# Inverting the delta rule's triangles in four row units, and merging their blocks in four queue steps

## The chip, the cores and the metric

One core of a Trainium2 chip runs the whole network once. The metric is the time of one execution on the device, in microseconds (us), as the median of several runs.

## What is computed

The network has two decoder layers on 256 tokens of width 2048. The first layer is a gated DeltaNet layer with 16 heads, the second attends differentially with a shared K/V; each ends with an MLP. The change lies in the DeltaNet layer, whose core the reference writes as

```python
lower = jnp.where(strict, jnp.einsum('bhnid,bhnjd->bhnij', k_beta, k) * decay, 0.0)
tri = lower + jnp.eye(CHUNK, dtype=lower.dtype)
sol = lax.linalg.triangular_solve(tri, rhs, left_side=True, lower=True, unit_diagonal=True)
```

The kernel does it with blocks of 128 tokens instead of 64: for each of 16 heads and 2 blocks there is one unit triangular matrix of 128x128 that has to be inverted and applied.

## The kernel before

Most of the program is weight products. A call of `gemm` multiplies the 256 tokens by 1024 columns of a weight matrix. The fp32 weights arrive in tiles of 128x1024 (`wr`), ScalarE rounds each to a high part `wh` (line 78), VectorE takes the remainder `wl` (line 79), and TensorE adds three products per tile, token block and half of the columns (lines 191 to 193, 128x512 each). One call has 16 weight tiles, 2 token blocks and 2 column halves, so 16 x 2 x 2 x 3 = 192 of these **weight matmuls**. Weight tiles are loaded four at a time; there are six buffers each for `wh` and `wl`.

The DeltaNet layer takes its heads in two halves of eight (`half(0)`, `half(1)`), and each half calls `gemm` for its k, q and v. All that is not a weight product is side work, and two queues hold it. `self.units` holds convolutions, scores and the like; `self.chain` holds steps that depend on each other: the inverse and the solve. `pump`, called after each token block of each four weight tiles, so once per 24 weight matmuls, takes one step of the chain and then `rate` units. The side work of a half therefore runs beside the weight products of its own v and of the next calls.

The inverse of a half, lines 571 to 644, is this chain: `inv_gather` copies the 32x32 diagonal blocks of 16 triangles (8 heads, 2 token blocks) through DRAM to 64 partitions; three empty steps; `inv_rows` inverts them there by forward substitution, two VectorE instructions per row (lines 593 and 600), 31 rows, in six units of up to six rows; `inv_scatter` writes the results back through DRAM into the diagonal of `Z` (lines 608 and 611, GpSimd's DMA queue); two empty steps; `inv_flip` transposes `Z` to `Y` (line 614); one empty step; and `inv_merge` puts pairs of blocks together, 32 to 64 and 64 to 128, in one step. For each pair it multiplies by `U` (line 630), copies the product from PSUM with ScalarE (line 631), multiplies again (line 634), and negates into `Y` with VectorE (line 635); for the first pairs a third product goes to `Z` (lines 641, 642). The products touch 32 or 64 rows and columns of the 128x128 array: a quarter or a smaller block of it, given by where the operands lie.

After the merge come two `solve` steps of four heads each: a product with `Y` (line 655), a ScalarE copy (656), a product (660), a VectorE subtraction (661), a product (664), a copy (665), and then the output products (670, 672), of which ScalarE sums the squares (677).

A scheduler of the framework turns this into one fixed order of instructions per engine when the program is built: it follows the order of the code, and by its own estimate of times it lets instructions that it thinks ready go ahead. The hardware runs each engine's instructions in that order, and an instruction that has to wait holds up all behind it on its engine.

Of the kernel before, what the change touches and what calls it, by code (L numbers as in the profile page):

```python
# [14 lines left out]
ALU = mybir.AluOpType  # L15
# [3 lines left out]
P = 128  # L19
# [3 lines left out]
KD = D // P  # L23
DFF = 8192
C = 1024
G = 512
# [9 lines left out]
class Trunk:  # L36
# [292 lines left out]
    @staticmethod  # L329
    def ends(n):  # L330

        return [5, 5, 6] if n == D // C - 1 else None
# [45 lines left out]
    def gated_deltanet(self, x, w_in, conv_w, a_log, dt_bias, norm_w, w_out, g, b, out=None):  # L378
# [6 lines left out]
        nc = self.nc  # L385
        v_ = nc.vector
        NH, DK, HH = 16, 128, 8
# [198 lines left out]
        def inv_rows(hf, j0, j1):  # L586
            Gp = hf["inv"][:64, :C].rearrange("p (j i) -> p j i", j=32)
            X = hf["inv"][:64, C:].rearrange("p (i c) -> p i c", i=32)
            for j in range(j0, j1):
                n = 31 - j  # L590
                t0 = j % 2 * 256
                t = hf["t"][:64, t0 : t0 + n * (j + 1)].rearrange("p (i c) -> p i c", i=n)
                v_.tensor_tensor(
                    t,
                    Gp[:, j, j + 1 :].unsqueeze(2).broadcast_to([64, n, j + 1]),
                    X[:, j : j + 1, : j + 1].broadcast_to([64, n, j + 1]),
                    op=ALU.mult,
                )
                xs = X[:, j + 1 :, : j + 1]
                v_.tensor_tensor(xs, xs, t, op=ALU.subtract)  # L600

        def inv_scatter(hf):
            X = hf["inv"][:64, C:].rearrange("p (i c) -> p i c", i=32)
            hf["Z"] = self.blk()
            nc.gpsimd.memset(hf["Z"], 0.0)
            Zv = hf["Z"].rearrange("p (n c) -> p n c", c=P)
            buf = self.dram.tile([4, 2 * HH, 32, 32], F32, name="g_inverses")
# [4 lines left out]
        def inv_flip(hf):  # L612
            hf["Y"] = self.blk()
            v_.transpose(hf["Y"], hf["Z"])

        def inv_merge(hf):

            Z = hf["Z"].rearrange("p (n c) -> p n c", c=P)
            Y = hf["Y"].rearrange("p (n c) -> p n c", c=P)
            U = lambda n: hf["U1"][:, n] if n < HH else hf["UA2"][:, 0, n - HH]  # L620
            mm = nc.tensor.matmul
            for w, r0 in ((32, 0), (32, 64), (64, 0)):
                a, b_ = slice(r0, r0 + w), slice(r0 + w, r0 + 2 * w)
                per = G // w
                for n0 in range(0, 2 * HH, per):
                    N = range(n0, n0 + per)
                    cs = lambda n: slice((n - n0) * w, (n - n0 + 1) * w)
                    tp, ts = self.ps(), self.sm()
                    for n in N:
                        mm(tp[b_, cs(n)], U(n)[a, b_], Z[a, n, a], start=True, stop=True)  # L630
                    nc.scalar.copy(ts[b_], tp[b_])
                    yp = self.ps()
                    for n in N:
                        mm(yp[a, cs(n)], ts[b_, cs(n)], Y[b_, n, b_], start=True, stop=True)
                    v_.tensor_scalar(
                        Y[a, n0 : n0 + per, b_], yp[a].rearrange("p (n c) -> p n c", c=w), -1.0, None, op0=ALU.mult
                    )
                    if w == 32 and r0 == 0:
                        zp = self.ps()
                        for n in N:  # L640
                            mm(zp[b_, cs(n)], Y[b_, n, b_], ts[b_, cs(n)], start=True, stop=True)
                        v_.tensor_scalar(
                            Z[b_, n0 : n0 + per, a], zp[b_].rearrange("p (n c) -> p n c", c=w), -1.0, None, op0=ALU.mult
                        )

        def solve(hf, gi, H):

            Y = hf["Y"].rearrange("p (n c) -> p n c", c=P)
            rv = hf["r"]
# [38 lines left out]

        def start_inverse(hf):
            rest = [(lambda *a: None, (hf,))]  # L690
            rows = [(lambda hf, j=j: inv_rows(hf, j, min(j + 6, 31)), (hf,)) for j in range(0, 31, 6)]
            self.chain.extend([(inv_gather, (hf,))] + rest * 3 + rows)
            self.chain.extend([(inv_scatter, (hf,))] + rest * 2 + [(inv_flip, (hf,))] + rest + [(inv_merge, (hf,))])

        def start_solve(hf, H):
            self.chain.extend((solve, (hf, g_, H)) for g_ in range(NG))
# [1 line left out]
        def half(hh):  # L698
            hf, H = {}, hh * HH
# [38 lines left out]
            for name, c0, ct in (("k", D, 16), ("q", 0, 0), ("v", 2 * D, 32)):  # L738
                pre = None
                if hh == 0 and name == "k":  # L740
                    pre = constants
                if hh == 0 and name == "q":
                    pre = gates
                self.gemm(KD, self.cols(w_in, c0 + H * DK), self.x_stat, ev_for(name, ct + H), pre=pre, rate=2)

        def gate(n):
            def ev(gi, t, ps):
# [9 lines left out]
            return ev  # L757

        half(0)
        half(1)  # L760
        for n in range(2):
            self.gemm(
# [204 lines left out]
```

## Time and profile before

| what | value |
|---|---|
| median of 3 runs | 2448.11 us (2443.59 to 2451.93) |
| the profiled execution's own time | 2446.75 us |
| its span in the profile | 2445.0 us |
| TensorE busy | 2406.5 us, 98% |
| VectorE busy | 1494.4 us, 61% |
| ScalarE busy | 1080.3 us, 44% |
| GpSimd busy | 48.3 us, 2% |
| mean granted clock of TensorE | 0.995 |

In the views, PE is TensorE's matmuls, PEld its weight loads, DVE VectorE, ACT ScalarE, POOL GpSimd, SP SyncE. The DeltaNet layer's six calls for k, q, v of both halves lie between about 11 and 301 us (half 0 and k, q of half 1) and up to 365 us (v of half 1); z follows up to 484 us. The merge and solves of half 0 stand from 262.8 to 293 us, those of half 1 from 440.8 to 478 us. A small fp32 product shows as two records.

### The profile page before, as it was taken

The page shows a single profiled execution, that of the slowest core. Times are in us where ns is not written, and L with a number is a line of the kernel's source. Part 1 is how long each engine was busy: PE and PEld are TensorE (multiplying, and loading weights), DVE is VectorE, ACT ScalarE, POOL GpSimd, SP SyncE. Part 2 cuts the span into 40 slices and gives each one's busy share as a digit, 9 for nine tenths or more (in the row PEclk, how much of TensorE's full clock was granted, in tenths as well). Part 3 has the DMA queues.
Part 4 walks back from the last instruction along what each step waited for, and adds up shares of the span by engine and source line. Part 5 has one row for each costly group of instructions (what it writes and reads, how often), then busy time and mean ns, then how long its engine had stood idle before and what let it go on. Part 6 is the DMA issues. An engine that isn't in the chain of part 4 may idle for free.

```text
span 2445.0 us, 30450 instructions
## 1 busy us (share of the span) xinstructions
PE 2406.5 (98%) x11492; PEld 1976.3 (81%) x11492; DVE 1494.4 (61%) x2348; ACT 1080.3 (44%) x1474; POOL 48.3 (2%) x79
## 2 busy tenths in 40 slices
PE   8999999999999999999999999999999999999997
PEld 6888888787888888888887877777888888888886
DVE  4789789557545554545557565766754545554556
ACT  4545445434433443534443454544343443443442
POOL 0010020000000000000000000000000000000001
PEclk9999999999999999999999999999999999999999
DMA  6545445464565556565554545555455555656553
GB/s 231 156 134 174 123 132 178 155 236 159 182 203 190 181 191 212 180 216 178 201 193 145 191 144 167 161 173 198 143 186 196 186 193 177 219 182 214 184 195 121
DMA packets 120212, 438.85 MB, mean 179 GB/s; under 512 B 13760, under 2 KB 13792, under 8 KB 119040
## 3 DMA queue, kind: packets, MB, share of 16 engines
q1 hardware_dynamic: 115920, 420.79, 52.1%
q0 software_dynamic: 2560, 11.13, 1.5%
q10 hardware_dynamic: 1584, 4.98, 0.5%
q8 instruction: 90, 1.47, 0.2%
q14 instruction: 58, 0.48, 0.1%
HBM read 433.70 MB, written 3.15 MB: 179 GB/s over the span
## 4 chain that ended last, share of the span: by engine, by line
PE 90%; DVE 5%; DMA 2%; issue 1%; ACT 1%; SPq 0%; ACTq 0%; DVEq 0%; POOLq 0%
PE acc L191 27%; PE acc L192 27%; PE acc L193 27%; PE ps L221 3%; DVE wl L79 1%; PE ps L832 1%; DMA wr<-in_gdn_w_in_dram 1%; PE ps L563 1%; ACT wh L78 1%; DMA wr<-in_shared_w_kv_dram 1%; PE ps L498 1%; PE ps L860 0%; PE ps L871 0%; DVE blk L282 0%; DVE blk L600 0%
## 5 line engine op out<-in xcount | busy, mean ns | idle before, releaser
L79 DVE TENSOR_TENSOR wl<-wr,wh 128x1024 fp32r<-128x1024 f32 x785 | 951.2, 1222 | 670.1 <-ACT wh L78 627.6
L78 ACT CAST wh<-wr 128x1024 fp32r<-128x1024 f32 x785 | 817.1, 1053 | 914.6 <-PE acc L193 748.3
L191 PE MATMUL acc<-wh,xhl 128*128 128x512 f32 x1860 | 737.0, 396 | 0.0
L192 PE MATMUL acc<-wl,xhl 128*128 128x512 f32 x1860 | 731.0, 393 | 0.1
L193 PE MATMUL acc<-wh,xhl 128*128 128x512 f32 x1860 | 729.0, 392 | 0.0
L191 PE MATMUL acc<-wh,blk 128*128 128x512 f32 x1280 | 499.3, 390 | 0.0
L193 PE MATMUL acc<-wh,blk 128*128 128x512 f32 x1280 | 498.6, 390 | 0.0
L192 PE MATMUL acc<-wl,blk 128*128 128x512 f32 x1280 | 498.5, 389 | 0.0
L191 PEld LDWEIGHTS acc<-wh,xhl 128*128 128x128 f32 x1860 | 351.0, 189 | 70.9 <-issue 1.7
L193 PEld LDWEIGHTS acc<-wh,xhl 128*128 128x128 f32 x1860 | 350.1, 188 | 71.7
L192 PEld LDWEIGHTS acc<-wl,xhl 128*128 128x128 f32 x1860 | 350.9, 189 | 69.4 <-issue 1.0
L193 PEld LDWEIGHTS acc<-wh,blk 128*128 128x128 f32 x1280 | 240.3, 188 | 50.2
L191 PEld LDWEIGHTS acc<-wh,blk 128*128 128x128 f32 x1280 | 240.3, 188 | 49.6
L192 PEld LDWEIGHTS acc<-wl,blk 128*128 128x128 f32 x1280 | 240.4, 188 | 49.3
L310 DVE SCALAR_TENSOR_TENSOR blk<-blk,acc 128x512 f32<-128x512 f32 x80 | 54.6, 684 | 71.3 <-PE acc L193 71.3
L221 PE MATMUL ps<-ident,sm 128*128 128x128 f32 x512 | 81.3, 275 | 2.1 <-DVE sm L882 1.7
L221 PEld LDWEIGHTS ps<-ident,sm 128*128 128x128 f32 x512 | 61.3, 140 | 26.8 <-PE acc L193 7.5
L78 ACT CAST blk<-ps 128x512 fp32r<-128x512 f32 x80 | 46.8, 585 | 70.2 <-PE ps L221 70.2
L362 DVE TENSOR_TENSOR sm<-sm 128x512 f32<-128x512 f32 x64 | 44.1, 691 | 50.5 <-ACT sm L361 50.1
L79 DVE TENSOR_TENSOR blk<-ps,blk 128x512 fp32r<-128x512 f32 x80 | 54.9, 686 | 30.1 <-ACT blk L78 30.1
L361 ACT ACTIVATE sm<-acc 128x512 f32<-128x512 f32 x64 | 38.3, 599 | 63.3 <-PE acc L193 60.4
L484 DVE SCALAR_TENSOR_TENSOR sm<-blk,g_cw,sm 128x255 f32<-128x255 f32 (+2 forms) x144 | 60.9, 475 | 0.0
(209 smaller groups left out, 1123.5 us busy)
## 6 DMA issues: line engine op xcount, KB each, us to landing
wr<-in_mlp_w_up_dram SPq DMA_DIRECT2D x256, 512.0 KB, 4.7
wr<-in_mlp_w_down_dram SPq DMA_DIRECT2D x256, 512.0 KB, 5.1
wr<-in_gdn_w_in_dram SPq DMA_DIRECT2D x128, 512.0 KB, 4.3
wr<-in_shared_w_kv_dram SPq DMA_DIRECT2D x64, 512.0 KB, 5.2
wr<-in_gdn_w_out_dram SPq DMA_DIRECT2D x32, 512.0 KB, 5.5
wr<-in_diff_w_q_dram SPq DMA_DIRECT2D x32, 512.0 KB, 4.6
wr<-in_diff_w_o_dram SPq DMA_DIRECT2D x32, 512.0 KB, 4.6
blk<-in_ln_g_dram POOLq DMA_DIRECT2D x4, 1024.0 KB, 7.3
```

The source lines that it names most:

```text
L78: self.nc.scalar.copy(hi, src)
L79: (engine or self.nc.vector).tensor_tensor(lo, src, hi.bitcast(F32), op=ALU.subtract)
L191: mm(ps, xh, wh[:, c], start=(k == 0), stop=False)
L192: mm(ps, xh, wl[:, c], start=False, stop=False)
L193: self.last = mm(ps, xl, wh[:, c], start=False, stop=(k == nk - 1))
L221: self.nc.tensor.transpose(pt[:, i], src[:, i * P : (i + 1) * P], self.ident)
L310: self.nc.vector.scalar_tensor_tensor(rc, rc, alpha, ps, op0=ALU.mult, op1=ALU.add)
L361: self.nc.scalar.activation(a, ps, AF.Relu)
L362: self.nc.vector.tensor_tensor(a, a, a, op=ALU.mult)
L484: v_.scalar_tensor_tensor(y[:, i, d:], u[:, : T - d], w(j), y[:, i, d:], op0=ALU.mult, op1=ALU.add)
L498: nc.tensor.matmul(pn[:, c : c + 1], sq[:, o : o + P], col1, start=True, stop=True)
L563: mm(p1[:, j], kT[:, n, :P], m[:, n], start=True, stop=True)
```

## The change

It does four things. The rows are inverted in four units of up to eight rows instead of six of up to six. The merge is four steps of the chain instead of one: step 0 multiplies by `U` for both pairs of 32 and copies, step 1 does the second products and the negations, steps 2 and 3 do the same for 64. Within a step two sets of products, with a PSUM tile each, are written in turn: for 32 the two sets lie in different quarters of the array, for 64 they are the two token blocks, in one quarter. The empty step ahead of the merge goes. And during the calls for v, `pump` takes three units instead of two.

```diff
--- before.py
+++ after.py
@@ -613,35 +613,51 @@
             hf["Y"] = self.blk()
             v_.transpose(hf["Y"], hf["Z"])
-        def inv_merge(hf):
-            Z = hf["Z"].rearrange("p (n c) -> p n c", c=P)
-            Y = hf["Y"].rearrange("p (n c) -> p n c", c=P)
+        def inv_merge(hf, step):
+            mm = nc.tensor.matmul
+            Z = lambda n: hf["Z"][:, n * P : (n + 1) * P]
+            Y = lambda n: hf["Y"][:, n * P : (n + 1) * P]
             U = lambda n: hf["U1"][:, n] if n < HH else hf["UA2"][:, 0, n - HH]
-            mm = nc.tensor.matmul
-            for w, r0 in ((32, 0), (32, 64), (64, 0)):
-                a, b_ = slice(r0, r0 + w), slice(r0 + w, r0 + 2 * w)
-                per = G // w
-                for n0 in range(0, 2 * HH, per):
-                    N = range(n0, n0 + per)
-                    cs = lambda n: slice((n - n0) * w, (n - n0 + 1) * w)
-                    tp, ts = self.ps(), self.sm()
-                    for n in N:
-                        mm(tp[b_, cs(n)], U(n)[a, b_], Z[a, n, a], start=True, stop=True)
-                    nc.scalar.copy(ts[b_], tp[b_])
-                    yp = self.ps()
-                    for n in N:
-                        mm(yp[a, cs(n)], ts[b_, cs(n)], Y[b_, n, b_], start=True, stop=True)
-                    v_.tensor_scalar(
-                        Y[a, n0 : n0 + per, b_], yp[a].rearrange("p (n c) -> p n c", c=w), -1.0, None, op0=ALU.mult
-                    )
-                    if w == 32 and r0 == 0:
-                        zp = self.ps()
-                        for n in N:
-                            mm(zp[b_, cs(n)], Y[b_, n, b_], ts[b_, cs(n)], start=True, stop=True)
-                        v_.tensor_scalar(
-                            Z[b_, n0 : n0 + per, a], zp[b_].rearrange("p (n c) -> p n c", c=w), -1.0, None, op0=ALU.mult
-                        )
+            w = 32 if step < 2 else 64
+            per = G // w
+            parts = [(0, 0), (64, 0)] if w == 32 else [(0, 0), (0, HH)]
+            ends = lambda r0: (slice(r0, r0 + w), slice(r0 + w, r0 + 2 * w))
+            cs = lambda m: slice(m * w, (m + 1) * w)
+            blocks = lambda p: p.rearrange("p (n c) -> p n c", c=w)
+            def negated(dst, rows, n0, cols, src):
+                d = dst.rearrange("p (n c) -> p n c", c=P)[rows, n0 : n0 + per, cols]
+                v_.tensor_scalar(d, blocks(src[rows]), -1.0, None, op0=ALU.mult)
+            ps = [self.ps() for _ in parts]
+            if step % 2 == 0:
+                hf["ts"] = [self.sm() for _ in parts]
+                for m in range(per):
+                    for (r0, n0), p in zip(parts, ps):
+                        a, b_ = ends(r0)
+                        mm(p[b_, cs(m)], U(n0 + m)[a, b_], Z(n0 + m)[a, a], start=True, stop=True)
+                for (r0, _), p, ts in zip(parts, ps, hf["ts"]):
+                    b_ = ends(r0)[1]
+                    nc.scalar.copy(ts[b_], p[b_])
+                return
+            for m in range(per):
+                for (r0, n0), p, ts in zip(parts, ps, hf["ts"]):
+                    a, b_ = ends(r0)
+                    mm(p[a, cs(m)], ts[b_, cs(m)], Y(n0 + m)[b_, b_], start=True, stop=True)
+            for (r0, n0), p in zip(parts, ps):
+                a, b_ = ends(r0)
+                negated(hf["Y"], a, n0, b_, p)
+            if w == 32:
+                a, b_ = ends(0)
+                zp, ts = self.ps(), hf["ts"][0]
+                for m in range(per):
+                    mm(zp[b_, cs(m)], Y(m)[b_, b_], ts[b_, cs(m)], start=True, stop=True)
+                negated(hf["Z"], b_, 0, a, zp)
         def solve(hf, gi, H):
@@ -688,9 +704,9 @@
         def start_inverse(hf):
             rest = [(lambda *a: None, (hf,))]
-            rows = [(lambda hf, j=j: inv_rows(hf, j, min(j + 6, 31)), (hf,)) for j in range(0, 31, 6)]
+            rows = [(lambda hf, j=j: inv_rows(hf, j, min(j + 8, 31)), (hf,)) for j in range(0, 31, 8)]
             self.chain.extend([(inv_gather, (hf,))] + rest * 3 + rows)
-            self.chain.extend([(inv_scatter, (hf,))] + rest * 2 + [(inv_flip, (hf,))] + rest + [(inv_merge, (hf,))])
+            self.chain.extend([(inv_scatter, (hf,))] + rest * 2 + [(inv_flip, (hf,))] + [(inv_merge, (hf, i)) for i in range(4)])
         def start_solve(hf, H):
             self.chain.extend((solve, (hf, g_, H)) for g_ in range(NG))
@@ -741,7 +757,7 @@
                     pre = constants
                 if hh == 0 and name == "q":
                     pre = gates
-                self.gemm(KD, self.cols(w_in, c0 + H * DK), self.x_stat, ev_for(name, ct + H), pre=pre, rate=2)
+                self.gemm(KD, self.cols(w_in, c0 + H * DK), self.x_stat, ev_for(name, ct + H), pre=pre, rate=3 if name == "v" else 2)
         def gate(n):
             def ev(gi, t, ps):
```

The chain of a half is 16 steps long before and after: two row units and an empty step go, three merge steps come.

What this does to the order shows at three places. The first is **TensorE, the end of half 0's merge and its first solve**. `acc` is the PSUM tile of the weight matmuls, `wh`, `wl` and `xhl` their operands, `ps` the PSUM tile of a side product. Before:

```order
L630 MATMUL ps<-blk 64x64 x8
L193 MATMUL acc<-wh,xhl 128x512
L191 MATMUL acc<-wh,xhl 128x512
L192 MATMUL acc<-wl,xhl 128x512
L193 MATMUL acc<-wh,xhl 128x512
L634 MATMUL ps<-blk,sm 64x64 x8
L655 MATMUL ps<-blk 128x128 x4
L191 MATMUL acc<-wh,xhl 128x512
L192 MATMUL acc<-wl,xhl 128x512
L193 MATMUL acc<-wh,xhl 128x512
L191 MATMUL acc<-wh,xhl 128x512
L660 MATMUL ps<-blk 128x128 x4
```

and after (line 643 was 630, 651 was 634, and from `solve` on 16 is added: 671 was 655, 676 was 660, 680 was 664, 686 was 670):

```order
L643 MATMUL ps<-blk 64x64 x16
L193 MATMUL acc<-wh,xhl 128x512
L651 MATMUL ps<-blk,sm 64x64 x16
L671 MATMUL ps<-blk 128x128 x4
L676 MATMUL ps<-blk 128x128 x4
L680 MATMUL ps<-blk 128x128 x4
L686 MATMUL ps<-blk 128x128 x5
L688 MATMUL ps<-blk 128x128
```

Before, four or six weight matmuls stand between each product and the next one of its chain. Now the last two merge steps and both solves of half 0 stand behind weight matmuls 959 and 960 of the kernel, that is at the end of the fifth call (q of half 1), with a single weight matmul among them; the second solve's rows read like the first's, and four transposes (line 221) follow. In half 1 three to ten weight matmuls still stand between them.

The second is **TensorE, the first merge steps of half 0** after the change:

```order
L643 MATMUL ps<-blk 32x32 x16
L191 MATMUL acc<-wh,xhl 128x512
L643 MATMUL ps<-blk 32x32 x16
...
L498 MATMUL ps<-g_col_114,sm 128x1 x4
L651 MATMUL ps<-blk,sm 32x32 x32
L659 MATMUL ps<-sm,blk 32x32 x16
```

The two sets of step 0 do not alternate in the built program: one weight matmul stands between them here, twelve in half 1. Those of step 1 do (x32). In half 1 the first set stands behind weight matmul 1436; before, the merge of half 1 began behind 1449.

The third is **VectorE, between two remainders `wl` that half 1's k needs**, while half 0's rows (593, 600) and the convolutions of its v (481, 484, 487) run. Before:

```order
L79 TENSOR_TENSOR wl<-wr,wh 128x1024
L593 TENSOR_TENSOR sm<-blk 64x220
L600 TENSOR_TENSOR blk<-blk,sm 64x22x10
L593 TENSOR_TENSOR sm<-blk 64x231
L600 TENSOR_TENSOR blk<-blk,sm 64x21x11
L593 TENSOR_TENSOR sm<-blk 64x240
L600 TENSOR_TENSOR blk<-blk,sm 64x20x12
L593 TENSOR_TENSOR sm<-blk 64x247
L79 TENSOR_TENSOR wl<-wr,wh 128x1024
```

and after:

```order
L600 TENSOR_TENSOR blk<-blk,sm 64x22x10
L484 SCALAR_TENSOR_TENSOR sm<-blk,g_cw,sm 128x254
L593 TENSOR_TENSOR sm<-blk 64x231
L484 SCALAR_TENSOR_TENSOR sm<-blk,g_cw,sm 128x253
L600 TENSOR_TENSOR blk<-blk,sm 64x21x11
L481 TENSOR_SCALAR sm<-blk,g_cw 128x256
L593 TENSOR_TENSOR sm<-blk 64x240
L484 SCALAR_TENSOR_TENSOR sm<-blk,g_cw,sm 128x255
L600 TENSOR_TENSOR blk<-blk,sm 64x20x12
L484 SCALAR_TENSOR_TENSOR sm<-blk,g_cw,sm 128x254
L593 TENSOR_TENSOR sm<-blk 64x247
L484 SCALAR_TENSOR_TENSOR sm<-blk,g_cw,sm 128x253
```

Rows and convolutions, which followed each other, now fall together, and the stretch of which these twelve are a part has 18 instructions between one remainder and the next.

## Rows read from the trace of the kernel before

**Rows 1.** The page's head and first part: span, busy time of each engine.
```profile
span 2445.0 us, 30450 instructions
PE 2406.5 (98%) x11492; PEld 1976.3 (81%) x11492; DVE 1494.4 (61%) x2348; ACT 1080.3 (44%) x1474; POOL 48.3 (2%) x79
```

**Rows 2.** Windows: stretch, length, then busy PE, PEld, DVE, ACT, POOL; clock; DMA.
```profile
180.00:200.00 20.00, 19.95 (x93) 15.95 (x92) 19.96 (x44) 13.13 (x23) 1.41 (x1) 1.00 0.55 172
...
280.00:300.00 20.00, 20.00 (x139) 17.66 (x138) 14.23 (x87) 9.87 (x41) 0.00 (x0) 1.00 0.10 29
...
420.00:440.00 20.00, 18.09 (x80) 14.64 (x78) 15.47 (x25) 8.76 (x9) 3.17 (x5) 1.00 0.76 230
440.00:460.00 20.00, 19.21 (x240) 15.80 (x241) 8.44 (x8) 5.93 (x7) 0.00 (x0) 0.91 0.43 132
```

**Rows 3.** PE's timeline, half 0's last merge product and first solve: start, length, instruction.
```profile
276.74 1.14 PE L634 MATMUL ps<-blk,sm 64*64 64x64 f32 x16
277.81 1.16 PE L655 MATMUL ps<-blk 128*128 128x128 f32 x8
278.73 0.47 PE L191 MATMUL acc<-wh,xhl 128*128 128x512 f32 x1
...
279.74 1.07 PE L660 MATMUL ps<-blk 128*128 128x128 f32 x8
280.56 0.47 PE L192 MATMUL acc<-wl,xhl 128*128 128x512 f32 x1
...
281.58 1.16 PE L664 MATMUL ps<-blk 128*128 128x128 f32 x8
```

**Rows 4.** The groups of instructions, by line: DVE and ACT, 180 to 500 us.
```profile
L79 DVE TENSOR_TENSOR wl<-wr,wh 128x1024 fp32r<-128x1024 f32 x86 | 103.5, 1215 | 24.2 <-ACT wh L78 23.5
L484 DVE SCALAR_TENSOR_TENSOR sm<-blk,g_cw,sm 128x255 f32<-128x255 f32 (+2 forms) x96 | 40.8, 475 | 0.0
L600 DVE TENSOR_TENSOR blk<-blk,sm 64x31 f32<-64x31 f32 (+15 forms) x62 | 20.5, 331 | 0.8
...
L635 DVE TENSOR_SCALAR blk<-ps 32x512 f32<-32x512 f32 (+1 forms) x8 | 5.5, 682 | 7.7 <-PE ps L634 7.6
...
L677 ACT ACTIVATE sm<-ps 128x128 f32<-128x128 f32 x32 | 8.4, 278 | 4.0 <-PE ps L672 2.7 <-PE ps L670 1.3
```

**Rows 5.** PE's timeline at half 1's first merge product, idle time in brackets.
```profile
437.70 0.39 PE L193 MATMUL acc<-wh,xhl 128*128 128x512 f32 x1
440.79 1.25 PE L630 MATMUL ps<-blk 32*32 32x32 f32 x32 [2.70 <-DMA blk<-g_inverses]
...
442.56 0.63 PE L192 MATMUL acc<-wl,xhl 128*128 128x512 f32 x1
442.98 0.63 PE L193 MATMUL acc<-wh,xhl 128*128 128x512 f32 x1
...
445.60 0.40 PE L191 MATMUL acc<-wh,xhl 128*128 128x512 f32 x1
445.83 0.40 PE L192 MATMUL acc<-wl,xhl 128*128 128x512 f32 x1
```

**Rows 6.** PE's timeline at two other waits.
```profile
247.00 1.05 PE L498 MATMUL ps<-g_col,sm 128*128 128x1 f32 x8 [0.86 <-ACT sm L492]
...
575.27 1.27 PE L221 MATMUL ps<-ident,blk 128*128 128x128 f32 x8 [2.31 <-issue]
```

**Rows 7.** Windows with the granted clock (the number before the last two), columns as in rows 2.
```profile
441.80:445.10 3.30, 3.30 (x12) 2.58 (x10) 0.47 (x1) 0.58 (x1) 0.00 (x0) 0.50 0.73 197
573.00:576.40 3.40, 1.13 (x8) 0.84 (x8) 3.38 (x6) 1.51 (x2) 0.00 (x0) 1.00 0.00 0
```

**Rows 8.** PE's timeline where two quarters meet, half 0: 32x32 products, five rows of one left out.
```profile
265.27 1.10 PE L634 MATMUL ps<-blk,sm 32*32 32x32 f32 x29
266.18 0.21 PE L641 MATMUL ps<-sm,blk 32*32 32x32 f32 x1
...
266.30 0.98 PE L641 MATMUL ps<-sm,blk 32*32 32x32 f32 x26
```

## The prediction, made before the changed kernel ran

> **What bounds the kernel now.** I read the page's first part, then windows of 20 us over the DeltaNet layer, then TensorE's timeline where the windows show less than a full engine. The page says that TensorE is busy for 2406.5 of 2445.0 us [rows 1]: a gain has to shorten TensorE's own list or its idle 38.6 us, and whatever makes it wait is paid in full. The windows show where the merge could matter. Half 0's solves run under a TensorE that is never idle (20.00 of 20.00 us, 280 to 300), while half 1's merge falls into two windows with 18.09 and 19.21 us busy [rows 2]. There the timeline shows the one large wait of this layer: the first merge product of half 1 waits 2.70 us for the DMA that brings the inverted blocks back, and behind it the weight matmuls come every 0.42 us instead of every 0.23 us [rows 5], at a granted clock of 0.50 (the 1.2 GHz level) for some 3.3 us [rows 7]. VectorE is full (19.96 of 20.00 us) where the rows are inverted [rows 2]; it makes the remainders that the weight matmuls need, so its order matters too.
>
> **The change part by part.** Since TensorE issues in a fixed order, the question at each product is what stands between it and the product that it depends on.
>
> *The cover of half 0's solves goes.* In the timeline of before TensorE has issued product 655 at 278.73, and its dependent 660 starts at 279.74: 1.01 us, filled with four weight matmuls. From 660 (280.56) to 664 (281.58) it is 1.02 us, again with four [rows 3]. These spans are a result draining, a ScalarE copy or a VectorE subtraction, and the way back; here the end of 655's records (277.81 + 1.16 = 278.97) is 0.77 us from the next start. After the change nothing stands in them, so what was cover becomes idle time. The links are: 643 to 651 of 64x64 with one weight matmul left (1.0 - 0.23 = 0.8), 651 to 671 over a negation of 0.68 us [rows 4] (1.0), and in each of two solves 671 to 676 and 676 to 680 (4 x 1.0): 5.8 us. The transposes behind the solves wait for ScalarE's copies, which stand behind the squares of line 677, four of 0.28 us each [rows 4]; of these 1.1 us I count 0.7, since part runs beside the output products. Sum **+6.5 us**. The lower bound is five links of 0.77 and one of 0.5, 4.4 us. The upper bound adds what can stand ahead in VectorE's and ScalarE's queues: a remainder of 1.2 us and a second negation of 0.7 us [rows 4], and as much again before the transposes, about 10 us.
>
> *Rows and convolutions fall together.* Shorter row units, three units per pump in v and a chain that starts a pump sooner put 18 VectorE instructions between two remainders, at 0.33 to 0.48 us each [rows 4] and with their own remainder of 1.2 us some 8.4 us. In that time TensorE has two spare weight tiles (six buffers, four in use) and the second token block of the current four: 24 + 12 weight matmuls of 0.23 us [rows 5], 8.2 us. So the remainder is at the edge. I take 1.0 us of waiting per half, **+2.0 us**. The bounds are 0 (before, no remainder is waited for in this layer) and 3 us per half.
>
> *The DMA wait of half 1.* By count the first product comes 13 weight matmuls sooner, 3.0 us, which would lengthen the wait to 5.7 us; but TensorE comes there some 7 us later by the two terms above, and the rows are done two pumps sooner on the chain. VectorE is what decides when they are done, and it is nearly full [rows 2], so I let the wait shrink by only **-1.0 us**, to 1.7. The bounds are -2.7 and +3.0. A wait of 2.31 us elsewhere left the clock at 1.00 [rows 6, 7], so a wait of 1.7 should leave it too: six matmuls at 0.42 instead of 0.23 us [rows 5], **-1.2 us** (bounds -1.2 and 0).
>
> *A convolution's wait.* The wait of 0.86 us at 247.00 [rows 6] stands before a product that now comes 40 weight matmuls later: **-0.9 us** (bounds -0.9 and 0).
>
> *Alternating quarters.* Within one quarter 32x32 records start every 31 ns (29 of them in 0.91 us). Where products of two quarters overlap, six starts take 0.12 us, 20 ns each [rows 8]. Only step 1 alternates, 64 records per half: 64 x 11 ns = 0.70 us, in two halves **-1.4 us**. Step 0's sets are built apart, and the steps for 64 share a quarter, so they gain nothing. The bounds are 0 (the six starts are an edge effect) and -2.0 (16 ns, twice the rate). Beside this row the Trainium skill, page "TensorE: Matmul & The Clock Gate", section "Wait — 56ns, not 53.3ns?", states that the distance between matmul starts never falls below about 25 ns however short they are. By that the term would be 64 x 6 ns x 2 = 0.8 us and the sum 0.6 us higher; the trace's 20 ns over six starts speaks against it, and I keep 20.
>
> *The rest.* The chain's three added pops cost no instruction. The DMAs of gather and scatter move to earlier pumps on GpSimd's queue, which is busy for 2% of the span [rows 1]; behind them stand only the score masks, so nothing. Step 0 now holds two `sm` tiles until step 1 has used them; six others serve the convolutions. If that is too few, it shows as late transposes, inside the upper bound of the first term.
>
> **Sum:** 6.5 + 2.0 - 1.0 - 1.2 - 0.9 - 1.4 = **+4.0 us**. The profiled execution took 2446.75 us, so it would take 2450.8; the median of the runs lies 1.4 us higher, so I predict a median of **2452.1 us**, +0.16%. A measurement of this kernel can tell about 0.3% (7.3 us) from no change, so this is no change, on the slow side: what the merge gives TensorE, it gives back at the end of half 0.
>
> **The rivals.**
> 1. *The clock falls in half 0's solves (slower).* For about 18 us TensorE would work in pieces of 1 us with waits of 1 us between them. The one wait of 2.70 us brought the clock to 0.50, one of 2.31 us did not [rows 5 to 7]. If one link grows past that, or the row of links counts together, the two solves' products, from 277.81 to 293 us with some 11 us of their own work, run up to twice as long: +7 to +10 us, or 2459 to 2462 us. For it: four to seven waits in a row, never seen in the trace of before. Against it: each is under half of the one that did it. It decides from a single wait of about 2.5 us on.
> 2. *VectorE becomes the bound in v (slower).* If the remainders are late by 3 us per half, at the upper bound, the sum is +8.0, 2456 us. For it: 19.96 of 20.00 us busy [rows 2]. Against it: the stretch fits within the buffers' 8.2 us but for a few tenths.
> 3. *The links are cheap and the DMA wait goes whole (faster).* With 4.4 for the links, 0 for the remainders, -2.7, -1.2, -0.9 and -2.0, the sum is -2.4 us, 2445.7. Faster than the bound would take links of nearly nothing, against [rows 3].
> 4. *The alternation does nothing*, and the 20 ns are an edge: the sum is +5.4, 2453.5 us, still no change.
>
> **How the numbers follow.** My forecast has 0.60, rival 1 0.12, rival 2 0.12, rival 3 0.08, rival 4 0.08. Rival 1 is slower; so are half of rival 2 and 0.04 of the forecast (links at 10 us): 0.22. Rival 3 as priced is no change; faster by over 0.3% I give 0.05, out of rival 3 with something more that the trace doesn't show. No change is left with 0.73. The range runs from rival 3's 2445 to 2460, the lower half of rival 1.
>
> **What would show it.** Right: TensorE idle by some 6 us in the stretch of half 0's merge and solves, in waits of about 1 us for the copies 672 and 681 and the subtraction 677 of the new numbering; lines 643 of half 1 waiting under 2.3 us with no fall of the clock; records of 651 (32x32) starting every 20 ns; one or two waits of about 1 us for `wl` in half 1's k and in z. Wrong: that stretch without idle time (the order did not bind), a granted clock of 0.50 in it, or waits on `wl` of several us.

## The result: slower by half a per cent, outside the range

The changed kernel takes 2463.34 us (median of 6 runs, 2460.76 to 2466.46) where the kernel before takes 2450.02 in the same comparison (6 runs, 2443.59 to 2453.47): a ratio of 1.005, 95% interval 1.0032 to 1.0067. I had forecast 2452.1 us, in a range up to 2460. The profiled execution took 2461.29 us against 2446.75 before, 14.5 us more; that difference is what has to be explained. The runs of the kernel before fall into two groups by TensorE's mean granted clock: of the 98 that ran beside the experiments below, 49 had 0.994 or more and took 2439.5 to 2450.2 us, 49 had 0.992 or less and took 2450.6 to 2466.2, and the profiled execution, at 0.995, is like the first.

The page's head and first part, after, answer to [rows 1]:

```profile
span 2459.6 us, 30445 instructions
PE 2411.2 (98%) x11492; PEld 1981.6 (81%) x11492; DVE 1494.5 (61%) x2348; ACT 1080.0 (44%) x1474; POOL 48.6 (2%) x79
```

The span grew by 14.6 us, of which 4.7 us are busy time of TensorE. With the same 11492 matmuls, that is matmuls that ran slower; the other 9.9 us are idle time. The windows, after (columns as in [rows 2]), show where:

```profile
280.00:300.00 20.00, 17.04 (x136) 15.12 (x135) 8.85 (x13) 8.52 (x18) 0.00 (x0) 0.83 0.45 132
300.00:320.00 20.00, 16.25 (x96) 14.29 (x96) 16.86 (x95) 9.17 (x35) 0.00 (x0) 0.91 0.01 2
420.00:440.00 20.00, 18.59 (x88) 15.06 (x87) 19.59 (x39) 9.46 (x12) 0.00 (x0) 1.00 0.60 186
440.00:460.00 20.00, 16.22 (x109) 12.96 (x108) 8.52 (x11) 5.81 (x6) 3.16 (x5) 0.91 0.66 206
```

From 280 to 300 us TensorE was busy for all 20.00 us before [rows 2]. Now it is busy for 17.04, and the granted clock of that window is 0.83: idle time and a slow clock in the same place. TensorE's timeline there, after, has half 0's 64x64 merge products and its two solves (weight matmuls and output products left out):

```profile
284.11 2.08 PE L643 MATMUL ps<-blk 64*64 64x64 f32 x32
...
286.79 2.08 PE L651 MATMUL ps<-blk,sm 64*64 64x64 f32 x32 [0.18 <-ACT sm L646]
...
290.19 1.27 PE L671 MATMUL ps<-blk 128*128 128x128 f32 x8 [1.33 <-DVE blk L635]
292.14 2.08 PE L676 MATMUL ps<-blk 128*128 128x128 f32 x8 [0.68 <-ACT blk L672]
295.00 2.07 PE L680 MATMUL ps<-blk 128*128 128x128 f32 x8 [0.78 <-DVE blk L677]
...
301.93 1.16 PE L676 MATMUL ps<-blk 128*128 128x128 f32 x8 [0.81 <-ACT blk L672]
304.26 1.65 PE L680 MATMUL ps<-blk 128*128 128x128 f32 x8 [1.17 <-DVE blk L677]
...
311.49 0.66 PE L221 MATMUL ps<-ident,sm 128*128 128x128 f32 x4 [1.77 <-ACT sm L722]
```

The solve links, which had four to six weight matmuls between their ends before (two of them stand in [rows 3]), now have a wait in brackets (0.68, 0.78, 0.81, 1.17), and so have the second 64x64 products (0.18), the first product of the first solve (1.33) and the transposes behind the solves (1.77): 6.7 us together. And the eight records of a solve step take 2.08 us (L676 at 292.14) where they take 1.16 (L676 at 301.93) at full clock. Two windows laid over the fall of the clock, after:

```profile
291.10:297.90 6.80, 5.35 (x24) 4.76 (x23) 1.46 (x2) 1.17 (x2) 0.00 (x0) 0.50 0.44 143
304.80:308.20 3.40, 3.40 (x18) 3.40 (x17) 2.00 (x10) 1.08 (x5) 0.00 (x0) 0.50 0.01 2
```

At a clock of 0.50 (1.2 GHz) TensorE worked for 5.35 + 3.40 = 8.75 us; at full clock that would be half, so by this estimate the fall cost 4.4 us. The remaining waits, in the list of TensorE's waits from 20 to 620 us, after (line, cause, total, times, longest):

```profile
PE ps L643 <- DMA blk<-g_inverses: 3.8, 1, 3.8
PE ps L221 <- issue: 2.7, 1, 2.7
PE acc L192 <- DVE wl L79: 2.0, 2, 1.1
...
PE ps L221 <- DVE sm L487: 1.5, 2, 1.0
PE ps L221 <- DVE sm L768: 1.4, 1, 1.4
```

The sum against the prediction's terms (us):

| term | predicted | measured | from |
|---|---|---|---|
| cover of half 0's solves | +6.5 | +6.7 | the seven brackets |
| the clock in that place | 0 | +4.4 | half of 8.75, an estimate |
| remainders `wl` | +2.0 | +2.0 | list of waits |
| transposes that wait for VectorE (L487, L768) | 0 | +2.9 | list, none before |
| half 1's wait for the inverse blocks | -1.0 | +1.1 | 3.8 less 2.70 [rows 5] |
| the clock behind that wait | -1.2 | 0 | fell for 3.4 us again |
| L498's wait at 247.00 | -0.9 | -0.9 | gone, against [rows 6] |
| alternating products | -1.4 | -1.6 | below |
| sum | +4.0 | +14.6 | span: +14.6 |

That the sum meets the span to a tenth is luck. All these terms lie ahead of weight matmul 1537, the first behind the DeltaNet layer's z, and there the changed kernel is already 16.1 us behind: TensorE is idle for 11.4 us more, about as the terms have it, but busy for 4.7 us more where they explain 2.8. The rest of the program gives 1.5 us back, in pieces of both signs, the largest -3.7 us between weight matmuls 6000 and 8000.

### The profile page after: what moved, and what is told of

The parts are those of the page before. It is cut to its first block, busy times and chain, and to the rows that moved or that the text cites. A ratio compares the mean times of both kernels' runs of the same rounds, so it can differ in the third digit from the quotient of the medians.

```text
span 2459.6 us, 30445 instructions
## 1 busy us (share of the span) xinstructions
PE 2411.2 (98%) x11492; PEld 1981.6 (81%) x11492; DVE 1494.5 (61%) x2348; ACT 1080.0 (44%) x1474; POOL 48.6 (2%) x79
## 3 DMA queue, kind: packets, MB, share of 16 engines
HBM read 433.70 MB, written 3.15 MB: 178 GB/s over the span
## 4 chain that ended last, share of the span: by engine, by line
PE 77%; DVE 4%; DMA 2%; issue 1%; ACT 1%; POOL 0%; ACTq 0%; POOLq 0%; DVEq 0%; SPq 0%
PE acc L191 24%; PE acc L193 24%; PE acc L192 24%; PE ps L221 2%; DVE wl L79 1%; PE ps L848 1%; PE ps L876 0%; DMA wr<-in_gdn_w_in_dram 0%; DMA wr<-in_shared_w_kv_dram 0%; PE ps L887 0%; DMA wr<-in_mlp_w_up_dram 0%; ACT wh L78 0%; DVE sm L593 0%; DVE blk L283 0%; DVE blk L282 0%
## 5 line engine op out<-in xcount | busy, mean ns | idle before, releaser
L221 PE MATMUL ps<-ident,sm 128*128 128x128 f32 x512 | 81.2, 275 | 6.3 <-ACT sm L722 1.8
L221 PEld LDWEIGHTS ps<-ident,sm 128*128 128x128 f32 x512 | 61.5, 140 | 30.7 <-PE acc L193 8.0
```

The source lines that it names most:

```text
L221: self.nc.tensor.transpose(pt[:, i], src[:, i * P : (i + 1) * P], self.ident)
```

## The experiments

For each kernel one row is shown that can be compared: the window from TensorE's 768th to its 975th weight matmul, which holds half 0's merge and solves (start and end, length, busy PE, ..., granted clock as the third number from the end). Before and after:

```profile
229.09:305.38 76.29, 75.41 (x580) 62.93 (x579) 60.04 (x173) 37.18 (x77) 3.17 (x5) 1.00 0.44 130
```
```profile
230.81:316.76 85.95, 78.93 (x580) 67.06 (x579) 60.94 (x165) 38.27 (x79) 3.17 (x5) 0.94 0.43 129
```

It is 9.7 us longer after, two thirds of the whole loss.

### Which part of the change does it

LINKS, the theory that this trace suggests, says that half 0's solves without cover are most of the loss, and that the row units of eight put them there. What it and its rivals expect stands in each text. Beside these four kernels the kernel before took 2452.85 us.

**Rows in six again**, all else as changed:

```diff
-inv_rows(hf, j, min(j + 8, 31)) ... range(0, 31, 8)
+inv_rows(hf, j, min(j + 6, 31)) ... range(0, 31, 6)
```

> The changed kernel (2463.3 us) with its rows in six units of up to six, as before; three units per pump in v and the merge in four steps stay. Theory LINKS (the loss is half 0's last merge steps and solves, which units of eight rows bring to the end of a weight call, where no weight matmul covers their waits and the clock falls): some 10 us come back, 2453 us, no granted clock below 1.00 and under 2 us of waits between 255 and 320 us. Theory VECTOR (three units per pump in v and longer row units bunch VectorE's work, so remainders and transposes come late): the rate stays, so 2460 us or more. Theory SPLIT (the four separate merge steps cost it): unchanged, 2463 us.

Measured: 2452.38 us, ratio 0.999 (0.9975 to 1.0005). The window:

```profile
230.79:307.00 76.21, 74.64 (x580) 62.91 (x579) 57.25 (x153) 37.20 (x77) 3.17 (x5) 0.98 0.43 128
```

As short as before, with the merge in four steps and rate 3. The 0.98 is a fall of the clock for 3.4 us at 242.4, behind a wait of 1.38 us at line 498; from 255 to 320 us there is none, as LINKS said. `wl` is waited for 2.1 us here too, so what a fuller VectorE costs is real, but it is not the main loss.

**Rate 2 in v**, all else as changed:

```diff
-rate=3 if name == "v" else 2
+rate=2
```

> The changed kernel with two units per pump in v, as before; rows in units of eight and the merge in four steps stay. LINKS: half 0's solves still stand at the end of a weight call without cover, so only the waits for remainders go: 2460 us, with a granted clock under 1.00 between 280 and 320 us. VECTOR: most of the loss goes, 2452 us. SPLIT: 2463 us.

Measured: 2460.42 us, ratio 1.0033 (1.0018 to 1.0048): the loss stays, and in the profile no `wl` is waited for. The window is 13.1 us longer than before's, with the clock at 0.50 from 282.5 us for 20.5:

```profile
229.44:318.82 89.38, 81.18 (x580) 69.47 (x579) 60.55 (x165) 37.31 (x77) 3.17 (x5) 0.89 0.39 124
```

**Rows of eight alone**, in the kernel before (the first diff, backwards):

> The kernel before (2450.0 us) with its rows in four units of eight, nothing else of the change. LINKS: the merge in one step and the solves of half 0 now stand at the end of a weight call, and lose their cover: 2459 to 2461 us, with waits of some 8 us and a fall of the clock between 280 and 320 us. VECTOR: some 3 us of late remainders, 2453 us. SPLIT: 2450 us, since the merge is as before.

Measured: 2464.68 us, ratio 1.0045 (1.0027 to 1.0063). One changed number brings nearly the whole loss, with the old merge:

```profile
228.72:318.05 89.33, 81.72 (x580) 69.87 (x579) 60.12 (x165) 37.67 (x77) 3.17 (x5) 0.90 0.40 124
```

**Rate 3 alone**, in the kernel before:

> The kernel before with three units per pump in v, nothing else of the change. LINKS: half 0's solves keep their cover; two or three us from late remainders and transposes, 2452 to 2453 us. VECTOR: 2458 us or more. SPLIT: 2450 us.

Measured: 2453.2 us, ratio 1.0001 (0.9985 to 1.0017). Its profile shows 1.5 us of waits for `wl` and its window is 0.7 us longer than before's; the medians do not differ.

So LINKS holds for most of the loss: in these kernels some 11 us come and go with the row units, whatever the merge and the rate. A smaller part is VECTOR's, and the clock of the kernel before hides it in the medians: at a mean clock of 0.994 or more, 14 of its 33 runs took 2446.5 us in the median, rows in six (all 12 runs) 2452.4, and rate 3 alone (4 of 12 runs) 2450.2. At an equal clock three units per pump cost some 4 us alone and up to 6 with the new merge.

### Is the clock a part of the loss, and what of the merge?

Beside the next four kernels the kernel before took 2448.47 us.

**Cover for half 0's links** by products that nothing reads:

```diff
+def fill(p):
+    for _ in range(4 if H == 0 else 0):
+        mm(p, ones, self.xhl[:, 0, 0, 0:4], start=True, stop=True)
 p2 = ps4()
+fill(p2)
```

(the same ahead of the third product, and ahead of the first solve's first)

> The changed kernel, with 20 extra products of 128x512 in half 0's two solves, each four of them ahead of a product that waits there (671, 676, 680). They multiply ready operands into the PSUM tile that the waiting product overwrites, so they add work that the reference does not need and change no output: 20 x 0.23 = 4.6 us, in about 5 us of idle time. CLOCK (part of the loss of half 0's stretch is the clock's fall behind the waits, not the waits): no granted clock under 1.00 between 280 and 320 us, the stretch from weight matmul 768 to 975 is 3 to 5 us shorter than in the changed kernel although TensorE does more, and the time is some 4 us less, about 2459 us. WAITS ALONE (the waits explain it, the clock costs nothing): the stretch is as long as before or up to 2 us longer, the time 2463 to 2465 us.

Measured: 2459.98 us, ratio 1.0038 (1.0021 to 1.0055). This interval overlaps the changed kernel's (1.0032 to 1.0067), so the time decides nothing. Its profile had the clock at 1.00 from 280 to 320 us, as CLOCK said, but at 0.50 twice earlier, from 251.7 for 6.8 us and from 272.2 for 3.4 us, behind 32x32 merge products, so that the window was as long as after's (86.37 us). A kernel with three products per place, further down, ran beside the changed kernel.

**The merge in four steps, alternating, alone** (rows in six, rate 2):

```diff
-rest + [(inv_merge, (hf,))]
+[(inv_merge, (hf, i)) for i in range(4)]
```

> The kernel before with its third part alone changed: the merge in four chain steps with alternating products and without the empty step; rows in six units and rate 2 as before. In the built order half 0's solves then keep their weight matmuls between the links (they stand at weight matmuls 936 to 989), but both solves of half 1 stand at the end of the last z call (1536) without any. COVER (what costs is a link that has nothing between its ends, wherever it stands): half 0's stretch within 2 us of before; half 1's, 1400 to 1728, longer by 4 to 8 us; 2455 to 2460 us. MERGE (the four steps are what costs, wherever the solves stand): half 0's stretch from 768 to 975 also longer by over 5 us. If neither: within 2 us of before.

Measured: 2458.62 us, ratio 1.0028 (1.0009 to 1.0048). Half 0's window has no clock under 1.00 and is 8.1 us shorter, of which most is work that moved behind it (529 records instead of 580; by weight matmul 1344 the kernel is level with before, +0.5 us). Half 1's stretch, 1400 to 1536, is 8.6 us longer, and to 1728, as the expectation has it, 10.9, more than the 4 to 8 expected. Its solves have the same waits as half 0's had after the change, to the hundredth; from TensorE's timeline of this kernel, and a window around all four waits:

```profile
478.89 1.16 PE L680 MATMUL ps<-blk 128*128 128x128 f32 x8 [0.78 <-DVE blk L677]
...
484.43 1.16 PE L676 MATMUL ps<-blk 128*128 128x128 f32 x8 [0.81 <-ACT blk L672]
486.76 1.16 PE L680 MATMUL ps<-blk 128*128 128x128 f32 x8 [1.17 <-DVE blk L677]
```
```profile
476.00:493.00 17.00, 11.16 (x91) 10.21 (x89) 11.95 (x58) 8.11 (x40) 0.00 (x0) 1.00 0.26 88
```

COVER holds: what a link waits is what stands between its ends, in either half. But here the same waits left the clock at 1.00. Not all of the 8.6 us is that: the wait for the inverse blocks grew to 5.2 us.

**The alternating products alone**: all four steps in one step of the chain, the empty step kept.

```diff
-rest + [(inv_merge, (hf,))]
+rest + [(lambda hf: [inv_merge(hf, i) for i in range(4)], (hf,))]
```

> The kernel before with the merge's products written in the new, alternating order, but all four steps in one chain step after the empty step, rows in six units, rate 2: the part of the change that was to help, alone. ALTERNATION HELPS: records of 32x32 in two quarters start every 16 ns, so 64 to 128 records per half save 15 ns each, 2 to 4 us in both halves, and the solves stay covered: 2448 to 2451 us against 2453 for the kernel before on such a chip (ratio 0.998 to 0.999), at the edge of what five rounds tell. ALTERNATION IS GIVEN BACK (the merge ends in a wait anyway): ratio 1.000. In both the wait for the inverse blocks in half 1 stays near 2.7 us.

Measured: 2446.46 us, ratio 0.9982 (0.9967 to 0.9997). The median is lower, but what the products give is mostly the clock: all 12 runs had a mean clock of 0.994 or more, and the 18 of the kernel before's 30 runs that had it took 2447.0 us in the median, 0.5 us more. Half 0's window is 2.5 us shorter (73.80 us). But half 1 hands most of that back, in the profile; TensorE's timeline:

```profile
441.61 1.88 PE L643 MATMUL ps<-blk 32*32 32x32 f32 x32 [4.87 <-DMA blk<-g_inverses]
```

TensorE arrives earlier and waits 4.87 us instead of 2.70 [rows 5]; the expectation of about 2.7 was wrong.

**The same with rows in units of five**, seven units, one step more in the chain:

```diff
-inv_rows(hf, j, min(j + 6, 31)) ... range(0, 31, 6)
+inv_rows(hf, j, min(j + 5, 31)) ... range(0, 31, 5)
```

> As the kernel with the alternating products alone, but with the rows in seven units of up to five, so that the chain is one step longer than before and half 1's merge starts a pump later. If the wait for half 1's inverse blocks is a matter of where the merge's first product stands, it falls under 1 us, the clock stays at 1.00 behind it, and the time is 3 to 6 us under the kernel before, 2447 to 2450 us where that takes 2453 (ratio 0.9975 to 0.999). If VectorE ends the rows as much later as the merge starts later, the wait stays at 2 to 3 us and the ratio is that of the alternating products alone.

Measured: 2438.43 us (8 runs, 2437.21 to 2440.75), ratio 0.9953 (0.9936 to 0.997): **faster than before by 0.5%** and than the changed kernel by 1%, more than expected. All 8 runs had a mean clock of 0.995 or more; the kernel before's runs at 0.994 or more took 2447.0 us, so 8.6 us remain at an equal clock. TensorE's timeline shows half 1's two first merge products with no wait at all, and a window of it the clock right behind them:

```profile
439.13 1.19 PE L643 MATMUL ps<-blk 32*32 32x32 f32 x32
...
441.58 1.24 PE L643 MATMUL ps<-blk 32*32 32x32 f32 x32
```
```profile
441.50:446.00 4.50, 4.42 (x40) 3.71 (x41) 3.19 (x2) 1.62 (x2) 0.00 (x0) 0.62 0.08 26
```

The wait is gone, yet the clock still fell for 3.4 us.

### The same questions, side by side

Beside these four kernels the kernel before took 2452.19 us.

**The changed kernel again:**

> The changed kernel itself, once more, beside the three others of this call on the same chip: it is what they are compared with. Expected: some 13 us over the kernel before, and a fall of the granted clock to 0.50 in half 0's solves again, of 10 to 20 us; a profile without one there would say that the fall is not the rule.

Measured: 2464.07 us, ratio 1.005 (1.003 to 1.007). The clock fell in half 0's solves again, for 6.8 us, less than the 10 to 20 expected (and for 3.4 us at 252.6):

```profile
230.17:317.32 87.15, 78.86 (x580) 66.97 (x579) 61.31 (x167) 38.16 (x79) 3.18 (x5) 0.94 0.43 128
```

**Three extra products per place** instead of four:

> As the filled kernel, with three instead of four extra products of 128x512 at each of five places ahead of 671, 676 and 680 in half 0's solves: 15 x 0.23 = 3.4 us of work into 4.8 us of waits (1.33 + 0.68 + 0.78 + 0.81 + 1.17). CLOCK: the median is 3 to 6 us below that of the changed kernel on the same chip and its mean granted clock higher, although TensorE has 3.4 us more to do. WAITS ALONE: the median is within 2 us of the changed kernel's, with the same mean clock.

Measured: 2460.68 us, ratio 1.0034 (1.0016 to 1.0052). That is 3.4 us less than the changed kernel on the same chip, with 3.4 us more work: none of its 12 runs is over 2462.1, and 9 of the changed kernel's 12 are at or over 2462.3. Its mean clock over the runs is mostly 0.994, the changed kernel's mostly 0.991 or 0.992. The window:

```profile
231.01:313.49 82.48, 79.62 (x595) 66.93 (x594) 61.39 (x165) 37.98 (x79) 3.18 (x5) 0.98 0.45 135
```

4.7 us shorter than the row above, and the clock did not fall in the solves. Of that, 1.6 us are waits for the inverse blocks at 249 and 252 us, which this profile of the changed kernel has and the filled one's has not, and 0.4 us is what filling takes from the waits (4.8 us of them became 3.4 us of work and 0.9 us of waits). The rest, some 2.7 us, is the clock's. CLOCK holds: covering waits that the critical path needs anyway, with work that nobody needs, gives time back, since the clock stays up.

**Rows in seven, rate 2**, all else as changed:

```diff
-min(j + 8, 31) ... range(0, 31, 8)
+min(j + 7, 31) ... range(0, 31, 7)
-rate=3 if name == "v" else 2
+rate=2
```

> The changed kernel with the rows in five units of up to seven instead of four of up to eight, and rate 2. In the built order both solves of half 0 then have weight matmuls between their links again (they stand at 919 to 949), and half 1's at 1508 to 1526 too. COVER: half 0's stretch from 768 to 975 is 1 to 3 us shorter than before although the merge has its four steps, no clock under 1.00 in it, half 1 as before; 2447 to 2451 us where before takes 2450 (ratio 0.998 to 1.001). FOUR STEPS COST BY THEMSELVES: that stretch stays over 5 us longer than before, ratio 1.002 or more.

Measured: 2445.59 us, ratio 0.9978 (0.9961 to 0.9995), 18.5 us under the changed kernel. With five units instead of four, half 0's solves have weight matmuls between their links again:

```profile
228.53:303.44 74.91, 73.49 (x580) 61.64 (x579) 55.89 (x149) 37.37 (x77) 3.18 (x5) 1.00 0.43 129
```

The four steps of the merge cost nothing by themselves. The gain over the kernel before is mostly the clock's: all 12 runs here had 0.994 or more, and the 17 of that kernel's 35 runs that had it took 2447.0 us in the median, 1.4 us more.

**Rows in five, the old merge:**

> The kernel before with nothing changed but the row units, seven of up to five, the merge as it was. If the gain of the kernel with rows of five came from where half 1's merge stands against its transfer, half 1's wait is under 0.5 us here too and the time is some 6 us under before (ratio 0.997), the other 3 to 4 us being the alternating products. If it came from the alternating products, the ratio is 0.999 to 1.000.

Measured: 2447.6 us, ratio 0.9985 (0.996 to 1.0011), runs from 2439.02 to 2457.43. As expected half 1's merge waits for nothing, yet the median gains little. The runs say why: seven of the 12 had a mean clock of 0.994 or more and took 2443.0 us in the median, 4.0 us under the kernel before's 17 such runs; the other five, at 0.992 or less, took 2450.8 to 2457.4. So the place of the merge alone is worth some 4 us, and only where the clock stays up. The 8.6 us of rows in five with alternating products are more than this and the 0.5 us of the products alone; that the products' gain, handed back at the transfer there, is kept here would explain it, but is not shown. The profiled execution is one of the five. Two windows of it, around the end of a run of 32x32 products in half 1:

```profile
445.00:451.40 6.40, 6.40 (x113) 5.48 (x111) 5.66 (x5) 3.15 (x3) 0.00 (x0) 1.00 0.21 73
451.50:471.90 20.40, 20.40 (x127) 16.32 (x128) 4.49 (x6) 3.32 (x5) 0.00 (x0) 0.50 0.25 82
```

TensorE is not idle for a moment in either, and its clock stands at 0.50 for all of the second. The wait is gone and in this execution the clock takes its place. With the alternating products, which shorten such runs, the same place had the fall of 3.4 us shown above.

## Why the prediction was wrong

**The failed step is the clock in half 0's solves**, my rival 1: my sum put it at 0, and it cost 4.4 us (an estimate, from 8.75 us of work at a clock of 0.50). I gave it 0.12 and wrote that it "decides from a single wait of about 2.5 us on". It decided without one: the longest of the seven waits is 1.77 us, and the first fall, at 291.1, came behind waits of 0.18 and 1.33 us and two runs of 64x64 products. I had two rows, a wait of 2.70 us with a fall and one of 2.31 without [rows 5 to 7], and drew a threshold of the length of one wait between them. But the first of these stands beside a run of 32x32 products, and the second was one draw of many. The same wait, of line 221, stands in all 14 profiles, 1.72 to 3.15 us long. In 12 of them, the changed kernel's among them, the clock fell within 2 us of its end, in the one with the shortest wait too; it stayed up in two, behind 2.31 us before and behind 3.00 us with rows in five. TensorE's timeline and a window of the merge in four steps alone, then of rows in five with alternating products:

```profile
586.10 1.27 PE L221 MATMUL ps<-ident,blk 128*128 128x128 f32 x8 [1.72 <-issue]
588.00:591.30 3.30, 3.30 (x9) 2.65 (x8) 2.99 (x13) 0.00 (x0) 0.00 (x0) 0.50 0.00 0
```
```profile
570.05 1.27 PE L221 MATMUL ps<-ident,blk 128*128 128x128 f32 x8 [3.00 <-issue]
570.00:573.40 3.40, 3.32 (x17) 2.56 (x18) 3.24 (x6) 1.17 (x2) 0.00 (x0) 1.00 0.00 0
```

Nor is a wait needed. With rate 2 in v the fall of half 0 began ahead of that place's first wait (0.66 us long, ending at 283.93), behind 32x32 products:

```profile
275.00:282.50 7.50, 7.50 (x126) 6.41 (x124) 4.97 (x9) 4.09 (x5) 0.00 (x0) 1.00 0.16 43
282.50:303.00 20.50, 17.37 (x107) 15.90 (x106) 5.72 (x8) 4.42 (x13) 0.00 (x0) 0.50 0.28 88
```

With rows of eight alone it began at 284.9, ahead of the first wait too. My other clause, that "the row of links counts together", is not shown either: the merge in four steps alone has the same four solve waits in half 1 with the clock at 1.00. So the runs show that in all four profiles with half 0's solves bare the clock fell there, and that between 280 and 320 us it did not in the two with extra products in the waits; what exactly brings it down stays open. The rival's price, 7 to 10 us, was too high here (4.4), as the output products ran mostly at full clock; by the same estimate the longer falls with rate 2 and with rows of eight alone cost 8.7 and 7.1 us. The measured time lies past the rival's 2459 to 2462 us because other terms grew.

**Cover, +6.5: right in the sum** (6.7), not link by link: I wrote 1.0 for 651 to 671 (1.33), 1.0 each for four solve links (0.68, 0.78, 0.81, 1.17), 0.8 for 643 to 651 (0.18) and 0.7 for the transposes (1.77). The four solve links were sized well (3.4 together); the other errors cancel, which is luck. The transposes were the cheap guess: none of the wait for the copies behind the squares is hidden.

**Remainders, +2.0: right** (0.85 and 1.13 us, in half 1's k and in z, as said). **Left out: the transposes behind VectorE.** I asked who waits for `wl`, but not who waits for the convolutions and z's products, which stand in the same fuller queue: L221 waited 2.9 us for them.

**The wait of half 1: wrong sign.** I let it shrink as TensorE would come later. VectorE came later too. Last row of the inverse on VectorE and the two transfers on GpSimd, before:

```profile
431.43 0.18 DVE L600 TENSOR_TENSOR blk<-blk,sm 64x31 f32<-64x31 f32 x1
```
```profile
431.91 0.53 POOL L608 DMA_DIRECT2D g_inverses<-blk  x1 [66.18 <-DVE blk L600]
435.66 2.63 POOL L611 DMA_DIRECT2D blk<-g_inverses  x4 [3.21 <-DMA g_inverses<-blk]
```

and after, with TensorE's last weight matmul and the product that waits:

```profile
442.59 0.18 DVE L600 TENSOR_TENSOR blk<-blk,sm 64x31 f32<-64x31 f32 x1
```
```profile
443.07 0.53 POOL L608 DMA_DIRECT2D g_inverses<-blk  x1 [64.34 <-DVE blk L600]
449.25 2.63 POOL L611 DMA_DIRECT2D blk<-g_inverses  x4 [5.65 <-DMA g_inverses<-blk]
```
```profile
449.53 0.39 PE L192 MATMUL acc<-wl,xhl 128*128 128x512 f32 x1
453.69 1.17 PE L643 MATMUL ps<-blk 32*32 32x32 f32 x32 [3.78 <-DMA blk<-g_inverses]
```

The rows end 11.2 us later, TensorE gets there 11.8 us later (449.92 against 438.09 [rows 5]), and from the rows' end to the product it takes 10.9 us instead of 9.2: the way through DRAM is 1.7 us longer, since the first transfer took 5.65 us to land instead of 3.21. So 11.2 + 1.7 - 11.8 = +1.1 us. With the wait the fall of the clock stayed too. Its price of 1.2 us was also low: in the trace of before seven weight matmuls run slow there, from 441.96 to 445.12 us, where seven of 0.23 us take 1.6.

**Alternation: right, its rate too cautious in half 0.** TensorE's timeline after, half 0:

```profile
267.00 1.11 PE L651 MATMUL ps<-blk,sm 32*32 32x32 f32 x58
267.92 0.21 PE L659 MATMUL ps<-sm,blk 32*32 32x32 f32 x1
```

58 starts in 0.92 us are 16 ns each, against 31 in one quarter [rows 8] and the 20 that I took. In half 1 the first 61 took 1.32 us, 22 ns each. Over 64 records that is 1.0 and 0.6 us. The floor of about 25 ns between matmul starts, which the Trainium skill gives (page "TensorE: Matmul & The Clock Gate", section "Wait — 56ns, not 53.3ns?"), does not hold here for records that alternate between quarters.

## What to carry to other kernels

Where a queue of side work is cut into new units, look up in the built order what stands between each product and the one it feeds: here units of eight rows lost 0.5%, and with units of seven and rate 2 the same four-step merge took 0.2% less than the kernel before. Cover has two prices: the wait, and the clock that falls with it; in these traces the second came behind runs of small products without a wait too, so a count of the waits alone does not price it. And a gain ahead of a transfer is handed back at the transfer, unless the place that waits for it moves too.

## What the runs showed of the hardware

- The granted clock fell to 0.50 for 20.5 us behind 32x32 products with TensorE busy throughout (rows in five, old merge), for 3.4 us behind two runs of 32 of them with no wait over 0.2 us (rows in five, alternating), and stayed at 1.00 behind single waits of 2.31 us [rows 6, 7] and 3.00 us; behind one of 1.72 us at the same place it fell. How long a fall lasts (3.4 to 20.5 us in these profiles) is open: no run here settles it.
- The clock accounts for most of the kernel before's own spread: beside the last four kernels its 35 runs took 2439.5 to 2449.6 us at a mean clock of 0.994 or more, and 2452.2 to 2464.6 at 0.992 or less. With the alternating products in one step, a change of nothing else, all 12 runs had 0.994 or more, and so had all 32 of rows in six, in seven and in five with these products and with weight matmuls left between the links. With the old merge and rows in five 7 of 12 had it. So the new order of the products keeps the clock up; that it does so because the runs of small products are shorter is likely, but was not tried by itself.
